# One hybrid decoder layer: a thinner order of seven-product pairs in one down projection, and two small f32 products in single-pass parts

## The chip, the cores and the metric

The kernel runs on one NeuronCore of a Trainium2 chip. The metric is the device time of one execution in microseconds. Before the change it is 1709.99 us, the median of three runs (1709.28 to 1711.11).

## The reference

One layer on x of 256 tokens by 2048, all in float32:

```
x = x + 0.5 * SwiGLU_1(RMSNorm(x))          # gate, up: 2048 x 5632; down: 5632 x 2048
h = RMSNorm(x);  z = h @ W_in               # columns: q,k (512 each), v (1024), g_low (16), r (1024) of the GLA group; q,k,v (1024 each) of the attention group
gate_logit = g_low @ gla_gate_up + gla_gate_bias          # 16 x 512
log_a = log_sigmoid(gate_logit) / 16
o_g = chunked gated linear attention(q, k, v, log_a)      # 4 heads, chunks of 64
      # within a chunk: b = cumsum(log_a);  k_state = k * exp(b_last - b)
o_a = dilated attention(q, k, v)                          # 8 heads, three branches
x = x + concat(o_g normed and gated, o_a) @ W_out
x = x + 0.5 * SwiGLU_2(RMSNorm(x))
```

The sum b_last - b, of the decays behind a position in its chunk, is what the kernel gets as a product of a constant "reversed" triangular matrix with log_a.

## The kernel before

**Products in parts.** A float32 operand of a large product is split in a high part, rounded to the type float32r that TensorE takes in a single pass, and a low part, the rest. A product is three matmuls: high by high, high by low, low by high. `split` (L115, L116) makes the parts: a copy on ACT for the high one, a subtraction on VectorE for the low one. Weights come from HBM as raw tiles of 1 MB (L221, by the SP queue, three buffers) that hold a k-pair: two k-tiles of 128 rows by 1024 columns. A raw tile is split in two weight tiles wh and wl of 128 x 1024 each, with four buffers for each name; `weights` keeps up to two of them ready beyond the one that it hands out (`AHEAD = 2`).

**A column pair** is two blocks of 512 output columns for both halves (128) of the tokens, four PSUM banks. It goes through all k-tiles in order. A plain k-tile is 12 matmuls of 512 columns (two token halves, two column blocks, three parts), a plain k-pair 24. In some pairs k-pairs are done by seven products instead of eight (the Strassen and Winograd scheme on the 2 x 2 blocks of tokens by k and k by columns), which is 21 matmuls. Such a seven needs sums of weight blocks, made on VectorE in `seven` (L243, L244, L247) and split like weights, and sums of the activations, made once in `seven_forms` (L322 to L328) and kept in `dforms`, in rooms lent from tiles hh and hl. Its products go to four further banks m, and after the last seven of a column pair `fold_into_xs` (L427 to L432) adds these up, in nine steps, one ahead of each half of a plain k-tile.

**The order** of plain (s) and seven (g) k-pairs in a column pair is a string, one letter a k-pair. A feed-forward block has 11 gate and up column pairs, then two down column pairs of 22 k-pairs each (`DOWN_ORDERS`):

```
DOWN_ORDERS = [_order("ssssssgssgssgsgsgsgsss"), _order("sgsgsgsgsgsgsgssgsssss")]
```

The list is the same in both feed-forward blocks; the first string is for the first column pair, the second for the second. `seven_pair` walks the string. Between the halves of plain k-tiles it runs small tasks from a list `later`, spread over a number of steps: the norm of the next stage, whose transposes go through POOL's queue (`norm_moved`, `move_squares`, L137), and activation sums of later sevens (`sums_of`, at given units by `extra`). In the second down column pair the parts of the norm that write to hh and hl are held back (`held`) until the last seven has been issued, and are then spread over 2 x (units left) - 6 steps. The scheduler that builds the program may move an instruction ahead of others on its engine where it reckons that it is ready earlier.

**The mix stage** follows the first feed-forward block and uses the memory that this frees. Its constants are loaded by POOL's queue (L601 to L610). Six column pairs (q and k, v of the attention; q with k, v, r of the GLA group) go through all 16 plain k-tiles each; `gate_low` (L753 on) comes between the third and the fourth. It accumulates the low-rank product g_low, with the weights' high part in rows 0 to 15 and their low part in rows 64 to 79 of one bank, copies it (L764, tile gl) and multiplies it by the gate matrix (L768, tile gup), which stands in rows 0 to 15 and 64 to 79 with zeros between, as plain f32. `scaled` (L794 on) multiplies the reversed triangle csq[:, 1] by the decays la as plain f32 (L800) and takes exponentials.

`t512` gives temporaries of 128 x 512, with four buffers.

Of the kernel before, what the change touches and what calls it, by code (L numbers as in the profile page):

```python
# [14 lines left out]
F32 = mybir.dt.float32  # L15
# [6 lines left out]
P = 128  # L22
# [21 lines left out]


FF_ORDERS = [_order("ssgsggss" if b in FF_THREE else "ssgssgss" if b in FF_SEVEN else "ssssssss") for b in range(FF // 512)]
DOWN_ORDERS = [_order("ssssssgssgssgsgsgsgsss"), _order("sgsgsgsgsgsgsgssgsssss")]
OUT_ORDERS = [_order("ssssssss"), _order("ssgsgsss")]


def layer_kernel(tc, x, xT, gains, gla_gate_up, gla_gate_bias, gla_out_norm, att_q_norm, att_k_norm,
# [6 lines left out]
    with ExitStack() as es:  # L58
# [17 lines left out]
                return [paux.tile([P, 512], F32, name="acc", tag="acc") for _ in range(2)] + [tp_bank() for _ in range(2)]  # L76
            return [pacc.tile([P, 512], F32, name="acc", tag="acc") for _ in range(4)]

        def t512(name):
            return cst.tile([P, 512], F32, name=name, tag="t512", bufs=4)  # L80

        def tp_bank():
            return ptp.tile([P, 512], F32, name="tp", tag="tp")
# [96 lines left out]
                    for part in ("plain", "last", "sums", "more") if seven else (0, 1):  # L180
                        yield w, cp * len(order) + kp, part

        jobs = [*jobs_of(w_ff1, FF_ORDERS), *jobs_of(w_dn1, DOWN_ORDERS)]
        jobs += [(w_mix, i, k) for i in range(3 * KT // 2) for k in range(2)] + ["low"]
        jobs += [(w_mix, i, k) for i in range(3 * KT // 2, 3 * KT) for k in range(2)]
        jobs += jobs_of(w_out, OUT_ORDERS)
        jobs += [*jobs_of(w_ff2, FF_ORDERS), *jobs_of(w_dn2, DOWN_ORDERS)]

        AHEAD = 2
        ready = []  # L190
# [140 lines left out]
        def seven_pair(acts, pairs, forms, odd, evac, fold, span=None, final=False, extra=None):  # L331

            cs, ms, folds = [acc_bank(), acc_bank(), tp_bank(), tp_bank()] if odd is None else four_banks(odd), None, []
            if odd is not None:
                order[0] = 4 * (1 - odd)
            units = [u for kp, seven in pairs for u in ([kp] if seven else [(2 * kp,), (2 * kp + 1,)])]
            lastseven = max(n for n, u in enumerate(units) if not isinstance(u, tuple))  # L340
            steps = span or 2 * sum(isinstance(u, tuple) for u in units)
            total = done = step = n = 0
            while n < len(units):
                u = units[n]
                if extra and n in extra:
                    extra[n]()
                if isinstance(u, tuple):
                    g = WBUF if final and n == len(units) - WBUF else 1
                    ws = [weights() for _ in range(g)]
                    last = n + g == len(units)  # L350
                    for t in range(NT):
                        step += 1
                        total = max(total, done + len(later))
                        go = min(max(-(-total * min(step, steps) // steps) - done, 0), len(later))
                        done += go
                        run_later(go)
                        if folds:
                            folds.pop(0)()
                        now = [acts[v[0]] for v in units[n:n + g]]
                        products(cs[2 * t:2 * t + 2], t, now, ws, n == 0, last, ((0,), (1,)) if g > 1 else ((0, 1),))  # L360
                        if last:
                            evac(t, [c.rearrange("p (a b) -> p b a", b=2) for c in cs[2 * t:2 * t + 2]])
                    n += g
                    continue
                start = ms is None
                if start:
                    ms = [acc_bank() for _ in range(4)] if odd is None else four_banks(1 - odd)
                seven_products(cs, ms, acts[2 * u:2 * u + 2], forms[u], start, n == lastseven)
                if start:
                    later.extend(second)  # L370
                    second.clear()
                if n == lastseven:
                    folds = fold([m.rearrange("p (a b) -> p b a", b=2) for m in ms])
                    if holding[0] == 1:
                        later.extend(held)
                        held.clear()
                        holding[0] = total = done = step = 0
                        steps = 2 * (len(units) - n) - 6
                n += 1
# [55 lines left out]
        def ffn(name, done, residual, extra=None, final=False):  # L435

            with tc.tile_pool(name=name, bufs=1, reuse_waits="tile") as fp:
# [73 lines left out]
                dforms = {kp + 1: [lent(hh, 2 * kp, 1), lent(hl, 2 * kp, 1)] for kp in range(4)}  # L511
                dforms[0] = [lent(hh, 12, 1), lent(hh, 14, 1)]
                dforms[5] = [lent(hl, 12, 1), lent(hl, 14, 1)]
                dforms.update({6 + i: [lent(a, 2 * i, 1) for a in (hh, hl)] for i in range(2)})

                def sums_of(kp):
                    seven_forms(dacts[2 * kp:2 * kp + 2], dforms[kp], t512("full"), t512("sums"))
# [8 lines left out]
                for cp in range(2):  # L526
                    def evac(t, ps, cp=cp):
                        for j in range(2):
                            c = 2 * cp + j
                            blk = xs[:, t, c * 512:(c + 1) * 512]  # L530
                            nc.vector.scalar_tensor_tensor(halves(blk), ps[j], 0.5, halves(blk), op0=ALU.mult, op1=ALU.add)  # L531
                            done(t, c, blk)

                    def fold(m, cp=cp):
                        return fold_into_xs(m, cp, urs, 0.5)

                    holding[0] = NT - cp
                    seven_pair(dacts, DOWN_ORDERS[cp], dforms, cp, evac, fold, span=28 if cp else 32, final=final and cp == 1,
                               extra={13 + 3 * i: lambda kp=6 + i: sums_of(kp) for i in range(2)} if cp else None)
                spare.close()  # L540


# [38 lines left out]
        with tc.tile_pool(name="mix", bufs=1, reuse_waits="tile") as mp:  # L581
# [1 line left out]
            oal = mp.tile([P, AH, S], F32R, name="oal")  # L583
            tabs = mp.tile([P, 4, NT, P], F32, name="tabs", tag="tabs")
            bm = mp.tile([P, 3 * P], F32, name="bm")
            csq = mp.tile([P, 3, P], F32, name="csq")
            gup = mp.tile([64 + RANK, 512], F32, name="gup")
            gon = mp.tile([P, GDV], F32, name="gon")

            def big(name, dt=F32):  # L590
# [12 lines left out]
            ld(gq[:, P:2 * P], att_k_norm.unsqueeze(0).to_broadcast([P, HD]))  # L603
            ld(bm[:, 0:P], c_mask[0:P, 0:P])
            ld(bm[:, P:3 * P], c_mask[P:2 * P, :])
            ld(csq, c_sq[:, P:4 * P].rearrange("p (a q) -> p a q", a=3))
            nc.gpsimd.memset(gup, 0.0)
            for r in (0, 64):
                ld(gup[r:r + RANK, :], gla_gate_up)
            ld(gon, gla_out_norm.unsqueeze(0).to_broadcast([P, GDV]))  # L610


# [140 lines left out]
            def gate_low():  # L753
                gb = acc_bank()
                for k in range(KT):
                    if k % 8 == 0:
                        w = weights()
                    nc.tensor.matmul(gb[:, :S], lhsT=w[:, k % 8, :], rhs=hh[:, k, :], start=k == 0, stop=False)
                    nc.tensor.matmul(gb[:, :S], lhsT=w[:, k % 8, :], rhs=hl[:, k, :], start=False, stop=k == KT - 1)
                gbias = t512("gbias")  # L760
                ld(gbias, gla_gate_bias.unsqueeze(0).to_broadcast([P, 512]))

                gl = mp.tile([64 + RANK, 3 * P], F32, name="gl", tag="sc", bufs=6)
                nc.vector.tensor_copy(gl[:, :S], gb[:64 + RANK, :S])  # L764
                lgs, ab = [t512("lg") for _ in range(NT)], e123[:, 0]
                for t, lg in enumerate(lgs):
                    b = tp_bank()
                    nc.tensor.matmul(b, lhsT=gl[:, t * P:(t + 1) * P], rhs=gup, start=True, stop=True)  # L768
                    nc.vector.scalar_tensor_tensor(lg, b, rt[:, t:t + 1], gbias, op0=ALU.mult, op1=ALU.add)
                    nc.vector.scalar_tensor_tensor(ab[:, t, :], lg, -1.0, lg, op0=ALU.mult, op1=ALU.min)  # L770
                nc.scalar.activation(ab, ab, AF.Exp)
                nc.scalar.activation(ab, ab, AF.Ln, bias=1.0)
                for t, lg in enumerate(lgs):
                    nc.vector.scalar_tensor_tensor(la[:, t, :], lg, 0.0, ab[:, t, :], op0=ALU.min, op1=ALU.subtract)
# [14 lines left out]
                nc.scalar.activation(e3[:, t, :], bt, AF.Exp)  # L789
                nc.vector.tensor_copy(dec[:, t, :], v(e3[:, t, :])[:, :, 63])  # L790

            kz = {}

            def scaled(t):  # L794
                for i, dsts in ((0, (e1, e3)), (1, (e2,))):
                    for d in dsts:
                        d = runs(d[:, t, :].rearrange("p (j q) -> p j q", j=4))
                        nc.vector.tensor_mul(d, in_order(moved[:, t, i, :]), d)
                b = tp_bank()
                nc.tensor.matmul(b, lhsT=csq[:, 1, :], rhs=la[:, t, :], start=True, stop=True)  # L800
                er = t512("er")
                nc.scalar.activation(er, b, AF.Exp)

                for c in (2 * t, 2 * t + 1)[:2 - t]:
                    one = csq[:, 2, 63 + 64 * (c % 2):64 + 64 * (c % 2)]
                    kz[c] = la[:, 0, :] if c == 0 else kg[:, t, :]
                    nc.vector.scalar_tensor_tensor(kz[c], kg[:, t, :], one, er, op0=ALU.mult, op1=ALU.mult)

# [17 lines left out]
            def intra(t):  # L826
# [6 lines left out]
                sm = sms["both"][:, t, :]  # L833
                nc.gpsimd.memset(sm, 0.0)
                v = lambda a: a.rearrange("p (h i) -> p h i", h=GH)
                nc.vector.copy_predicated(v(sm), csq[:, 2, :].bitcast(U32).unsqueeze(1).to_broadcast([P, GH, P]), v(b))
                sms[t] = sm

            later.extend([lambda: None] * 4 + [lambda h=h: both(values, h) for h in (4, 6)])
# [160 lines left out]
```

## Time and profile before

| | |
|---|---|
| median of three runs | 1709.99 us |
| profiled execution | 1710.49 us, span 1708.7 us |
| granted TensorE clock | 0.999 |
| TensorE busy | 1696.9 us, 99% of the span, 7932 instructions |
| weight loads busy | 1477.4 us, 86% |
| VectorE busy | 1472.8 us, 86% |
| ACT busy | 973.4 us, 57% |
| POOL busy | 506.2 us, 30% |
| HBM read | 354.57 MB |

The profile calls TensorE's matmuls PE and its weight loads PEld, VectorE DVE, ScalarE ACT, GpSimd POOL and SyncE SP. A matmul's busy time in the rows is longer than the distance to the next, since they overlap; what a matmul costs in a full stream is the distance from start to start. A plain f32 matmul stands in the rows as two instructions.

### The profile page before, as it was taken

The page shows a single profiled execution, that of the slowest core. Times are in us where ns is not written, and L with a number is a line of the kernel's source. Part 1 is how long each engine was busy: PE and PEld are TensorE (multiplying, and loading weights), DVE is VectorE, ACT ScalarE, POOL GpSimd, SP SyncE. Part 2 cuts the span into 40 slices and gives each one's busy share as a digit, 9 for nine tenths or more (in the row PEclk, how much of TensorE's full clock was granted, in tenths as well). Part 3 has the DMA queues.
Part 4 walks back from the last instruction along what each step waited for, and adds up shares of the span by engine and source line. Part 5 has one row for each costly group of instructions (what it writes and reads, how often), then busy time and mean ns, then how long its engine had stood idle before and what let it go on. Part 6 is the DMA issues. An engine that isn't in the chain of part 4 may idle for free.

```text
span 1708.7 us, 22402 instructions
## 1 busy us (share of the span) xinstructions
PE 1696.9 (99%) x7932; PEld 1477.4 (86%) x7932; DVE 1472.8 (86%) x1823; ACT 973.4 (57%) x1207; POOL 506.2 (30%) x1002
## 2 busy tenths in 40 slices
PE   9999999999999999999999999999999999999999
PEld 7888888888888878888888888888888888888887
DVE  6989999999899997577856688989998999899986
ACT  7656565555555555564654555556555655555553
POOL 0333334343400601064250034333333333420000
PEclk9999999999999999999999999999999999999999
DMA  8566656666666666567564457666666666666663
GB/s 347 211 232 225 218 210 236 212 235 216 235 245 223 216 220 226 195 231 243 190 217 169 151 198 249 231 234 210 235 224 229 223 215 219 222 247 232 220 235 135
DMA packets 85809, 378.63 MB, mean 222 GB/s; under 512 B 21393, under 2 KB 38801, under 8 KB 42689
## 3 DMA queue, kind: packets, MB, share of 16 engines
q1 hardware_dynamic: 50864, 350.25, 57.9%
q0 software_dynamic: 34112, 25.88, 5.4%
q8 instruction: 62, 1.02, 0.2%
q10 hardware_dynamic: 720, 1.07, 0.2%
q14 instruction: 51, 0.41, 0.1%
HBM read 354.57 MB, written 4.19 MB: 210 GB/s over the span
## 4 chain that ended last, share of the span: by engine, by line
PE 89%; DVE 5%; DMA 4%; issue 1%; POOL 0%; ACT 0%; DVEq 0%; SPq 0%; ACTq 0%; POOLq 0%
PE acc L281 19%; PE acc L283 19%; PE acc L279 19%; PE acc L305 5%; PE acc L306 5%; PE acc L304 5%; PE tp L283 4%; PE tp L281 4%; PE tp L279 4%; DVE wl L116 3%; DMA raw<-in_w_dn_dram 2%; PE tp L306 1%; PE tp L305 1%; PE tp L304 1%; DMA xs<-us 1%
## 5 line engine op out<-in xcount | busy, mean ns | idle before, releaser
L115 ACT ACTIVATE wh<-raw 128x1024 fp32r<-128x1024 f32 (+2 forms) x610 | 631.9, 1047 | 444.0 <-PE acc L283 207.0
L116 DVE TENSOR_TENSOR wl<-raw,wh 128x1024 fp32r<-128x1024 f32 (+1 forms) x608 | 733.1, 1215 | 127.0 <-ACT wh L115 124.3
L137 POOL DMA_DIRECT2D xs<-us x704 | 344.5, 497 | 545.6 <-DVE us L130 284.1
L283 PE MATMUL acc<-wh,hl 128*128 128x512 f32 x1192 | 359.3, 381 | 0.0
L281 PE MATMUL acc<-wl,hh 128*128 128x512 f32 x1192 | 358.8, 381 | 0.1
L279 PE MATMUL acc<-wh,hh 128*128 128x512 f32 x1192 | 347.9, 381 | 2.3 <-ACT wh L115 2.3
L279 PEld LDWEIGHTS acc<-wh,hh 128*128 128x128 f32 x1192 | 224.8, 189 | 35.4 <-ACT wh L115 3.5
L281 PEld LDWEIGHTS acc<-wl,hh 128*128 128x128 f32 x1192 | 225.1, 189 | 32.7 <-DVE wl L116 0.5
L283 PEld LDWEIGHTS acc<-wh,hl 128*128 128x128 f32 x1192 | 225.3, 189 | 32.2 <-issue 0.5
L115 ACT ACTIVATE wh<-xs 128x1024 fp32r<-128x1024 f32 x100 | 105.6, 1056 | 103.3 <-DVE xs L247 31.9
L116 DVE TENSOR_TENSOR wl<-xs,wh 128x1024 fp32r<-128x1024 f32 x100 | 120.4, 1214 | 2.7 <-ACT wh L115 2.6
L281 PE MATMUL acc<-wl,uh 128*128 128x512 f32 x368 | 113.1, 381 | 2.6 <-DVE wl L116 2.6
L283 PE MATMUL acc<-wh,ul 128*128 128x512 f32 x368 | 112.2, 379 | 0.0
L279 PE MATMUL acc<-wh,uh 128*128 128x512 f32 x368 | 106.2, 380 | 0.5 <-ACT wh L115 0.5
L137 POOL DMA_DIRECT2D hh<-us x128 | 62.1, 500 | 121.1 <-DVE xs L531 68.5
L243 DVE TENSOR_TENSOR xs<-raw 128x1024 f32<-128x1024 f32 x50 | 61.1, 1222 | 29.3 <-DMA raw<-in_w_ff_dram 29.2
L281 PEld LDWEIGHTS acc<-wl,uh 128*128 128x128 f32 x368 | 68.7, 189 | 15.1 <-DVE wl L116 5.6
L279 PEld LDWEIGHTS acc<-wh,uh 128*128 128x128 f32 x368 | 69.3, 189 | 11.1 <-ACT wh L115 1.3
L283 PEld LDWEIGHTS acc<-wh,ul 128*128 128x128 f32 x368 | 69.6, 189 | 9.9
L279 PE MATMUL tp<-wh,hh 128*128 128x512 f32 x200 | 61.6, 379 | 0.0
L281 PE MATMUL tp<-wl,hh 128*128 128x512 f32 x200 | 59.5, 379 | 0.0
L283 PE MATMUL tp<-wh,hl 128*128 128x512 f32 x200 | 59.5, 379 | 0.0
(326 smaller groups left out, 2540.0 us busy)
## 6 DMA issues: line engine op xcount, KB each, us to landing
raw<-in_w_ff_dram SPq DMA_DIRECT2D x175, 1024.0 KB, 5.1
raw<-in_w_dn_dram SPq DMA_DIRECT2D x88, 1024.0 KB, 4.9
raw<-in_w_mix_dram SPq DMA_DIRECT2D x48, 1024.0 KB, 5.0
raw<-in_w_out_dram SPq DMA_DIRECT2D x16, 1024.0 KB, 4.8
xs<-us POOLq DMA_DIRECT2D x704, 16.0 KB, 4.0
xs<-in_x_dram SPq DMA_DIRECT2D x2, 1024.0 KB, 9.5
xs<-in_x_dram POOLq DMA_DIRECT2D x2, 1024.0 KB, 5.9
hh<-us POOLq DMA_DIRECT2D x128, 16.0 KB, 3.7
```

Source lines behind the costliest of these rows:

```text
L115: nc.scalar.activation(dst_h, src, AF.Copy)
L116: nc.vector.tensor_sub(dst_l, src, dst_h.bitcast(F32))
L137: nc.gpsimd.dma_start(dst[32 * q:32 * q + 32, ..., r * n:(r + 1) * n], src[32 * r:32 * r + 32, ..., q * n:(q + 1) * n])
L243: nc.vector.tensor_add(room["sum"], b1, blocks[:, 1:3, :])
L279: nc.tensor.matmul(ps[j], lhsT=sh, rhs=alt(wh[:, j, :]), start=first and i == 0, stop=False)
L281: nc.tensor.matmul(ps[j], lhsT=sh, rhs=alt(wl[:, j, :]), start=False, stop=False)
L283: nc.tensor.matmul(ps[j], lhsT=sl, rhs=alt(wh[:, j, :]), start=False, stop=last and i == len(ws) - 1)
L304: nc.tensor.matmul(bank, lhsT=a[0], rhs=alt(ws[0][:, j, :]), start=start, stop=False)
L305: nc.tensor.matmul(bank, lhsT=a[0], rhs=alt(ws[1][:, j, :]), start=False, stop=False)
L306: nc.tensor.matmul(bank, lhsT=a[1], rhs=alt(ws[0][:, j, :]), start=False, stop=stop)
```

## The change

1. The second down column pair of the first feed-forward block gets an order of its own, with seven sevens instead of eight, and two plain k-pairs between them from the second one on. The other three down column pairs keep theirs. The set of activation sums that only the eighth seven used is no longer made there.
2. The gate matrix is loaded four times (rows 0, 32, 64, 96) into a temporary, copied to float32r, and in rows 96 to 127 replaced by its low part. The low-rank product gl gets four groups of 32 rows: the high part of the product, its low part, the high part of the product with the weights' low part, and the high part again. One single-pass matmul over 128 rows takes the place of a plain f32 one over 80 rows.
3. The reversed triangle becomes a float32r tile of its own, and the decays are split in high and low; two single-pass matmuls take the place of one plain f32 matmul, in both token halves. The constants are loaded in two pieces.

The fold's step gets a loop of one turn, which changes nothing.

```diff
-DOWN_ORDERS = [_order("ssssssgssgssgsgsgsgsss"), _order("sgsgsgsgsgsgsgssgsssss")]
+DOWN_ORDERS = {name: [_order("ssssssgssgssgsgsgsgsss"), _order(text)]
+               for name, text in (("ffn1", "sgsgssgssgssgssgssgsss"), ("ffn2", "sgsgsgsgsgsgsgssgsssss"))}
...
-        def t512(name):
-            return cst.tile([P, 512], F32, name=name, tag="t512", bufs=4)
+        def t512(name, dt=F32):
+            return cst.tile([P, 512], dt, name=name, tag="t512", bufs=4)
...
-                dforms.update({6 + i: [lent(a, 2 * i, 1) for a in (hh, hl)] for i in range(2)})
+                dforms.update({6 + i: [lent(a, 2 * i, 1) for a in (hh, hl)] for i in range(3)})
...
-                    seven_pair(dacts, DOWN_ORDERS[cp], dforms, cp, evac, fold, span=28 if cp else 32, final=final and cp == 1,
-                               extra={13 + 3 * i: lambda kp=6 + i: sums_of(kp) for i in range(2)} if cp else None)
+                    seven_pair(dacts, DOWN_ORDERS[name][cp], dforms, cp, evac, fold, span=28 if cp else 32, final=final and cp == 1,
+                               extra={at: lambda kp=6 + i: sums_of(kp) for i, at in enumerate((13,16,) if final else (13,))} if cp else None)
...
-            csq = mp.tile([P, 3, P], F32, name="csq")
-            gup = mp.tile([64 + RANK, 512], F32, name="gup")
+            csq = mp.tile([P, 2, P], F32, name="csq")
+            rev = mp.tile([P, P], F32R, name="rev")
+            gup = mp.tile([P, 512], F32R, name="gup")
...
-            ld(csq, c_sq[:, P:4 * P].rearrange("p (a q) -> p a q", a=3))
-            nc.gpsimd.memset(gup, 0.0)
-            for r in (0, 64):
-                ld(gup[r:r + RANK, :], gla_gate_up)
+            cs = c_sq[:, P:4 * P].rearrange("p (a q) -> p a q", a=3)
+            ld(csq, cs[:, 0::2, :])
+            ld(rev, cs[:, 1, :].bitcast(F32R))
+            full = t512("full")
+            nc.gpsimd.memset(full, 0.0)
+            for r in range(0, P, 32):
+                ld(full[r:r + RANK, :], gla_gate_up)
+            nc.scalar.activation(gup, full, AF.Copy)
+            nc.vector.tensor_sub(gup[96:P, :], full[96:P, :], gup[96:P, :].bitcast(F32))
...
-                gl = mp.tile([64 + RANK, 3 * P], F32, name="gl", tag="sc", bufs=6)
-                nc.vector.tensor_copy(gl[:, :S], gb[:64 + RANK, :S])
+                gl = mp.tile([P, 3 * P], F32R, name="gl", tag="sc", bufs=6)
+                nc.scalar.activation(gl[0:32, :S], gb[0:32, :S], AF.Copy)
+                nc.scalar.activation(gl[64:96, :S], gb[64:96, :S], AF.Copy)
+                nc.vector.tensor_copy(gl[96:P, :S], gl[0:32, :S].bitcast(F32))
+                nc.vector.tensor_sub(gl[32:64, :S], gb[0:32, :S], gl[0:32, :S].bitcast(F32))
...
+            def in_parts(t):
+                lhl[t] = [t512("l" + n, F32R) for n in "hl"]
+                split(*lhl[t], la[:, t, :])
...
+                in_parts(t)
                 b = tp_bank()
-                nc.tensor.matmul(b, lhsT=csq[:, 1, :], rhs=la[:, t, :], start=True, stop=True)
+                for i, a in enumerate(lhl.pop(t)):
+                    nc.tensor.matmul(b, lhsT=rev, rhs=a, start=i == 0, stop=i == 1)
```

More of the change, by code (lines that the diff above doesn't have):

```diff
@@ L181, in jobs_of @@
                         yield w, cp * len(order) + kp, part
-        jobs = [*jobs_of(w_ff1, FF_ORDERS), *jobs_of(w_dn1, DOWN_ORDERS)]
+        jobs = [*jobs_of(w_ff1, FF_ORDERS), *jobs_of(w_dn1, DOWN_ORDERS["ffn1"])]
         jobs += [(w_mix, i, k) for i in range(3 * KT // 2) for k in range(2)] + ["low"]
@@ L186, in layer_kernel @@
         jobs += jobs_of(w_out, OUT_ORDERS)
-        jobs += [*jobs_of(w_ff2, FF_ORDERS), *jobs_of(w_dn2, DOWN_ORDERS)]
+        jobs += [*jobs_of(w_ff2, FF_ORDERS), *jobs_of(w_dn2, DOWN_ORDERS["ffn2"])]
         AHEAD = 2
@@ L356, in seven_pair @@
                         run_later(go)
-                        if folds:
-                            folds.pop(0)()
+                        for _ in range(1):
+                            if folds:
+                                folds.pop(0)()
                         now = [acts[v[0]] for v in units[n:n + g]]
@@ L790, in decays @@
                 nc.vector.tensor_copy(dec[:, t, :], v(e3[:, t, :])[:, :, 63])
-            kz = {}
+            kz, lhl = {}, {}
+            def in_parts(t):
+                lhl[t] = [t512("l" + n, F32R) for n in "hl"]
+                split(*lhl[t], la[:, t, :])
             def scaled(t):
@@ L804, in scaled @@
                 for c in (2 * t, 2 * t + 1)[:2 - t]:
-                    one = csq[:, 2, 63 + 64 * (c % 2):64 + 64 * (c % 2)]
+                    one = csq[:, 1, 63 + 64 * (c % 2):64 + 64 * (c % 2)]
                     kz[c] = la[:, 0, :] if c == 0 else kg[:, t, :]
@@ L835, in intra @@
                 v = lambda a: a.rearrange("p (h i) -> p h i", h=GH)
-                nc.vector.copy_predicated(v(sm), csq[:, 2, :].bitcast(U32).unsqueeze(1).to_broadcast([P, GH, P]), v(b))
+                nc.vector.copy_predicated(v(sm), csq[:, 1, :].bitcast(U32).unsqueeze(1).to_broadcast([P, GH, P]), v(b))
                 sms[t] = sm
```

## The prediction

> **What bounds the kernel now.** I read the page's busy shares first, then windows over the stretches that the diff touches, then the waits and the chain in them, then groups by shape for durations. In the window rows the columns are the stretch, its length, and busy us with (instructions) for PE, PEld, DVE, ACT, POOL, then granted clock, DMA share and GB/s.
>
> ```profile
> PE 1696.9 (99%) x7932; PEld 1477.4 (86%) x7932; DVE 1472.8 (86%) x1823; ACT 973.4 (57%) x1207; POOL 506.2 (30%) x1002
> 200.00:440.00 240.00, 240.00 (x1114) 210.16 (x1113) 224.18 (x252) 141.12 (x158) 94.41 (x193) 1.00 0.65 224
> 561.00:673.00 112.00, 109.62 (x505) 94.67 (x504) 99.21 (x119) 62.44 (x75) 35.50 (x72) 1.00 0.67 223
> 600.00:640.00 40.00, 37.62 (x171) 31.64 (x170) 37.43 (x45) 22.27 (x26) 1.72 (x4) 1.00 0.62 220
> 600.00:610.00 10.00, 9.26 (x43) 7.82 (x42) 9.64 (x15) 4.91 (x6) 1.72 (x4) 1.00 0.60 207
> ```
>
> TensorE is never far from full: in the stall-free 200 to 440 us it starts 1113 matmuls of 512 columns in 240.00 us, 0.2156 us each. That pitch is my unit. 561 to 673 us is the second down pair of layer one (its 8x21 + 28x12 = 504 matmuls are the 504 weight loads of the row); at the pitch they take 108.7 us, so about 3.3 us of 112.0 are lost. All of it lies in 600 to 640 us: 170 x 0.2156 = 36.7 of 40.0 us. What ends last there:
>
> ```profile
> 601.74 0.70 PE L281 MATMUL acc<-wl,uh 128*128 128x512 f32 x2 [0.74 <-DVE wl L116]
> 612.83 0.70 PE L281 MATMUL acc<-wl,uh 128*128 128x512 f32 x2 [1.11 <-DVE wl L116]
> 623.34 0.70 PE L281 MATMUL acc<-wl,uh 128*128 128x512 f32 x2 [0.53 <-DVE wl L116]
> ...
> ACT wh L115 <- DVE raw L247: 23.6, 6, 4.8
> DVE wl L116 <- ACT wh L115: 8.7, 8, 1.4
> DVE urs L243 <- DMA raw<-in_w_dn_dram: 2.6, 4, 1.0
> ...
> 604.25 6.06 DMA raw<-in_w_dn_dram
> ```
>
> PE waits each time for a low half (wl) of a plain pair that stands behind a seven's sums on VectorE; ACT waits for VectorE's sums too (23.6 us in six waits), so VectorE feeds both. VectorE is busy 9.64 of 10 us where the first stall falls, and what it lacks is a raw weight buffer that comes free too late (the chain runs through a 6.06 us load).
>
> **Part 1, the order of the second down pair.** One seven becomes a plain pair. PE: 24 matmuls for 21, +3 x 0.2156 = +0.65 us; that is certain and on the path. The engines that feed it, by these rows of the same stretch:
>
> ```profile
> L116 DVE TENSOR_TENSOR wl<-raw,wh 128x1024 fp32r<-128x1024 f32 x45 | 54.2, 1219 | 8.8 <-ACT wh L115 8.7
> L243 DVE TENSOR_TENSOR urs<-raw 128x1024 f32<-128x1024 f32 x7 | 8.6, 1223 | 2.6 <-DMA raw<-in_w_dn_dram 2.6
> L116 DVE TENSOR_TENSOR hl<-raw,hl 128x512 fp32r<-128x512 f32 x7 | 4.8, 685 | 0.0
> L244 DVE TENSOR_TENSOR raw<-urs,raw 128x512 f32<-128x512 f32 x7 | 4.8, 684 | 0.0
> L247 DVE TENSOR_TENSOR raw<-raw 128x512 f32<-128x512 f32 x7 | 4.8, 684 | 0.0
> L427 DVE SCALAR_TENSOR_TENSOR xs<-urs,xs 128x512 f32<-128x512 f32 x4 | 2.7, 683 | 0.0
> L322 DVE TENSOR_TENSOR full<-uh,ul 128x256 f32<-128x256 f32 x4 | 1.5, 410 | 0.0
> L325 DVE TENSOR_TENSOR sums<-full 128x128 f32<-128x128 f32 x2 | 0.6, 284 | 0.0
> ```
>
> A seven costs VectorE 1.22 + 3 x 0.685 + 3 x 1.22 = 6.93 us, a plain pair 2 x 1.22 = 2.44. The old stretch alternates them: 9.37 us of VectorE under 45 x 0.2156 = 9.70 us of PE, 97%, before the sums of activations (2 x 0.41 + 4 x 0.28 + 0.69 = 2.64 us a time), the transposes of the norm and their halves are counted. So the backlog that eats PE's lead of prepared weights is forced. The new order has this beat only for its first two sevens, and from then on two plain pairs to a seven: 11.81 us of VectorE under 69 x 0.2156 = 14.88 us of PE, 79%, three us spare per beat. In all VectorE sheds 6.93 - 2.44 + 2.64 = 7.1 us (one set of activation sums goes too) of 99.2. The first stall comes only at 601.74, some forty us into the pair, and the relief starts with the fifth pair (its weights were being prepared near 576 us), so I expect all the stalls to go: -3.3 us. Bounds: 0 if the backlog outlives the change, -3.3 if none is left; I take -3.3, nearest to the 200 to 440 row, where VectorE at 224/240 = 93% let PE lose nothing. Late next is PE itself. The raw loads are as many as before, one a pair, so SP's queue is not moved.
>
> The end of the pair gets denser. Behind the last seven stood five plain pairs, now three: 72 matmuls, 15.5 us. Into them go nine fold steps (one ACT copy, eight VectorE operations of 0.68 = 5.5 us), two late halves of the norm (1.4 us) and six weight halves (7.3 us): 14.2 of 15.5 us. The norm pieces held back until the last seven must run in 8 steps instead of 16. Then come the rows of the seam:
>
> ```profile
> 640.00:657.00 17.00, 17.00 (x81) 14.88 (x80) 15.79 (x20) 9.65 (x11) 0.00 (x0) 1.00 0.65 227
> 657.00:673.00 16.00, 16.00 (x76) 14.02 (x75) 8.95 (x10) 6.57 (x7) 4.44 (x8) 1.00 0.78 258
> 673.00:691.00 18.00, 18.00 (x93) 15.85 (x92) 16.75 (x31) 11.24 (x19) 3.81 (x4) 1.00 0.61 216
> ```
>
> Today VectorE has seven us free just ahead of the mix stage and is 93% busy in its first 18 us. The new tail uses up most of that free time. What covers it is the lead: four weight tiles, one in use, three ahead, each 12 matmuls or 2.6 us of PE, so up to 7.8 us. If that cover goes, the price is the overhang of 0 to 2 us; I take 0.2.
>
> **Part 2, gate factor and reversed sums in single passes.** Today these are plain f32, and the chain of work shows them whole:
>
> ```profile
> 808.82 1.72 PE tp L768 x4
> 895.01 0.86 PE tp L800 x2
> 896.74 0.86 PE tp L800 x2
> ```
>
> Two gate products at 1.72/2 = 0.86 us and two reversed sums at 0.86 us. The gate's become one single-pass matmul each (128 rows hold all four part products): 2 x (0.86 - 0.2156) = -1.29 us. The sums become two each: 2 x (0.86 - 0.431) = -0.86 us. Together -2.15 us on PE. PE never waited around either place, so it comes off the end. The TensorE page of the Trainium skill (TensorE: Matmul & The Clock Gate, Back-to-back issue gap) gives about 131 ns for a sustained 512-column matmul beside the isolated 216; by 131 the change would give an estimated -1.46 - 1.20 + 0.39 = -2.26 us on PE instead of -1.50. The trace has 0.2156 over 1113 matmuls and decides.
>
> What the parts cost elsewhere, by the nearest rows:
>
> ```profile
> L116 DVE TENSOR_TENSOR hl<-hf,hh 128x512 fp32r<-128x512 f32 x16 | 10.9, 685 | 1.6 <-ACT hh L115 1.4
> L115 ACT ACTIVATE hh<-hf 128x512 fp32r<-128x512 f32 x16 | 9.9, 624 | 8.3 <-DVE hf L125 4.8 <-DVE hf L157 3.3
> L116 DVE TENSOR_TENSOR oal<-tp,oah 128x256 fp32r<-128x256 f32 x8 | 3.2, 421 | 6.0 <-ACT oah L115 6.0
> L115 ACT ACTIVATE oah<-tp 128x256 fp32r<-128x256 f32 x8 | 2.8, 383 | 3.9 <-PE tp L735 3.9
> 880.00:905.00 25.00, 25.00 (x131) 21.65 (x130) 15.92 (x21) 16.27 (x24) 11.06 (x21) 1.00 0.58 193
> 798.00:815.00 17.00, 17.00 (x92) 14.65 (x91) 11.17 (x12) 9.82 (x12) 5.46 (x11) 1.00 0.78 260
> ```
>
> Splitting the decays costs two ACT copies of 0.62 and two VectorE subtracts of 0.69 (1.25 and 1.37 us) near 895 us, where VectorE has 9 and ACT 8.7 of 25 us free: nothing, under weight splits that PE does not wait for. The small factor needs two ACT copies of 0.38 and one VectorE operation of 0.42 more, behind the accumulation of the low-rank product; engines 66% and 58% busy hide it, and a wait here would hold PE in order, but the product starts 4.5 us after the end of the copy that it reads (row below, and 808.82 above):
>
> ```profile
> 803.94 0.41 DVE L764 COPY gl<-acc 80x256 f32<-80x256 f32 x1
> 663.02 0.76 POOL L601 DMA_DIRECT2D rope<-in_c_rope_dram  x1 [61.30 <-PE tp L281]
> 666.43 0.55 POOL L607 MEMSET gup<- 80x512 f32 x1
> 680.80 1.04 POOL L609 DMA_DIRECT2D gup<-in_gla_gate_up_dram  x2
> gup<-in_gla_gate_up_dram POOLq DMA_DIRECT2D x2, 32.0 KB, 2.5
> ```
>
> The gate matrix now goes through a temporary: on POOL's queue three more transfers (two copies of the matrix, the constants in two pieces), some 1.6 us, behind which wait only the norm's small powers and the output gain, needed a pair later. New is that ACT (0.62) and VectorE (0.69) wait for four loads. POOL's queue gets going at 663.02 and reaches the memset at 666.43, so four loads of 0.52 can't be out before 669; placed as today's two (680.80) they are out at 682.9 and land 2.5 later, near 685 us. Whatever stands behind that ACT copy in its queue, weight splits above all, is held until then. From both sides: nothing if it is queued where its loads have landed, up to 14 us if it is queued at the top of the stage (a hold of 663 to 685 less the lead of 7.8). I take nothing, nearest to the rotary tables, which wait for loads of the same queue and stand at 676.9 us without idle time before them:
>
> ```profile
> 676.91 0.90 DVE L618 SCALAR_TENSOR_TENSOR tabs<-rope,gq 128x128 f32<-128x128 f32 x4
> ```
>
> The loop around the fold and the extra data type argument change nothing.
>
> **Sum.** +0.65 - 3.3 - 2.15 + 0.2 = -4.6 us. The profiled execution took 1710.49 (span 1708.7); it becomes 1705.9. The median of the three runs, 1709.99, is 0.5 below the profiled one, so for a median I give 1705.4.
>
> **Rivals.** (a) The stalls stay. For it: the load of a raw buffer is on the chain, and the first two sevens keep their old beat. Against: the load is late because VectorE is. Then only -1.5 is left: 1708.5. (b) A tail stall: the folds and held norm pieces in 8 steps meet the mix stage's 93% VectorE and PE runs out of prepared weights. For: 14.2 of 15.5 us. Against: the lead, and three spare us of VectorE in every beat ahead of it, into which pieces of the norm whose data is there can move. 1 to 3 us of new waits: 1706.2 to 1708.2, say 1707.2. (c) The other side: ACT is held by the gate matrix's loads at the head of the mix stage. It decides from a hold of 7.8 + 4.6 = 12.4 us: beyond that the kernel is slower; the full hold of 22 us gives 14 us on PE, 1719.6. Against it: today's loads and their readers are queued in the order in which they get ready. The clock is granted at 1.00 in every row above, with no PE wait over 1.11 us in this stretch. By the Trainium skill (same page, The HAM clock gate) an idle window of about 3.4 us halves the clock, so this rival would also show slower matmuls after the hold, an estimated 1 or 2 us more; no run here shows it. (d) The single passes save nothing because another engine ends last there: the windows at 798 and 880 have VectorE at 64 to 66%, so only 3%: 1707.5.
>
> **How the numbers follow.** Forecast 58% (1704.3 to 1706.5), (a) 18%, (b) 16%, (c) 5% (half of it short enough to end near 1710), (d) 3%. Two tenths of a per cent, 3.4 us, is about what this measurement can tell from no change: faster means under 1706.6. The forecast gives nearly all of its 58 to faster, (b) some 5 more: 0.62. Same: (a), the rest of (b), (d) and part of (c): 0.34. Slower: 0.04. The range for 8 in 10 takes the forecast, (b) and half of (a): 1703.9 to 1708.5.
>
> **What would show it.** In the second down pair 507 matmuls, no wait of PE for wl between 600 and 640 us, the pair 109.3 us long instead of 112; gate products and reversed sums at 0.22 and 0.43 us instead of 0.86; the mix stage's first pair without a PE wait, and ACT's copy into gup with little idle time before it. Wrong would make it: PE waits at the last three plain pairs or at the seam (b), an ACT wait for gup's load over 7 us (c), or waits of the old size at other sevens (a).

## The result

Eleven runs of each gave a median of 1705.25 us against 1710.54 for the kernel before; the ratio is 0.9968, with a 95% interval of 0.9960 to 0.9975. Two repetitions beside other experiments gave 0.9976 (0.9967 to 0.9985) and 0.9969 (0.9958 to 0.9981). The kernel is faster, by about 5 us. The profiled execution has a span of 1703.5 us instead of 1708.7.

First the busy shares of the changed kernel:

```profile
PE 1694.2 (99%) x7933; PEld 1478.2 (87%) x7933; DVE 1469.4 (86%) x1815; ACT 974.8 (57%) x1209; POOL 508.1 (30%) x1005
```

Its windows, columns as in the prediction:

```profile
561.00:673.00 112.00, 112.00 (x520) 98.07 (x520) 96.19 (x111) 64.60 (x77) 35.74 (x72) 1.00 0.67 228
600.00:640.00 40.00, 40.00 (x187) 35.04 (x186) 34.68 (x39) 22.47 (x24) 1.57 (x4) 1.00 0.57 204
```

In the same 112 us PE now starts 520 matmuls instead of 504 (the pair itself has 507, so the mix stage is already running in the last 2.7 us), and in 600 to 640 us it starts 186 instead of 170: 186 x 0.2156 = 40.1 us, nothing lost. VectorE went from 37.43 to 34.68 us there. Then the waits of 561 to 672 us (who waits for whom: us in total, times, longest):

```profile
DVE urs L244 <- DMA raw<-in_w_dn_dram: 8.7, 5, 2.1
DVE wl L117 <- ACT wh L116: 5.6, 9, 1.2
ACT wh L116 <- DVE raw L248: 3.9, 2, 2.1
```

Line numbers are higher than before by one or more. PE isn't in the list any more; ACT waits 3.9 us for VectorE's sums instead of 23.6. VectorE itself waits longer for raw tiles, 8.7 us instead of 2.6: it has become early, which costs nothing. The chain of work shows the two small products:

```profile
805.94 0.47 PE tp L779 x2
893.90 0.24 PE tp L817
894.78 0.23 PE tp L817
900.63 0.23 PE tp L817
901.31 0.23 PE tp L817
```

1.72 us have become 0.47, and twice 0.86 have become four times 0.23 or 0.24. Where the gate matrix is loaded and copied, the timeline has (start, length, instruction, idle time before it):

```profile
678.50 1.99 POOL L615 DMA_DIRECT2D full<-in_gla_gate_up_dram  x4 [0.29 <-POOL full L613]
686.18 0.61 ACT L616 ACTIVATE gup<-full 128x512 fp32r<-128x512 f32 x1
687.56 0.69 DVE L617 TENSOR_TENSOR gup<-full,gup 32x512 fp32r<-32x512 f32 x1
```

And its windows at the seam of the stages:

```profile
640.00:657.00 17.00, 17.00 (x80) 14.88 (x80) 14.18 (x16) 10.18 (x12) 0.00 (x0) 1.00 0.61 226
657.00:673.00 16.00, 16.00 (x76) 14.01 (x75) 13.84 (x18) 8.43 (x13) 4.67 (x8) 1.00 0.84 284
673.00:691.00 18.00, 18.00 (x93) 15.83 (x92) 15.56 (x29) 10.42 (x14) 5.27 (x7) 1.00 0.53 190
```

ACT has no idle time in front of the copy. VectorE's free seven us before the mix stage have shrunk to two (13.84 of 16.00 busy instead of 8.95), and PE loses nothing.

Since TensorE is full, the time is best laid out by the start of the first matmul of each column pair in the trace. Lengths in us from that start to the next pair's:

| | second down pair, layer one | pair with the gate product | the two pairs with the reversed sums | all other stages, sum of differences |
|---|---|---|---|---|
| before | 112.23 | 48.40 | 101.57 | |
| changed | 109.43 | 47.15 | 100.79 | |
| difference | -2.80 | -1.25 | -0.78 | -0.4 |

Before, both reversed sums fell in the first of their two pairs, and now one falls in each; the pairs are therefore taken together. The column pairs of the mix and output stages that hold no change, and the gate and up stages of layer two, agree to 0.02 us. The -0.4 comes from the gate and up stages at the start (-0.30), and from layer two's down pairs (+0.28 and -0.38), which differ as much between runs of one kernel.

### The profile page after: what moved, and what is told of

The parts are those of the page before. It is cut to its first block, busy times and chain, and to the rows that moved or that the text cites. A ratio compares the mean times of both kernels' runs of the same rounds, so it can differ in the third digit from the quotient of the medians.

```text
span 1703.5 us, 22406 instructions
## 1 busy us (share of the span) xinstructions
PE 1694.2 (99%) x7933; PEld 1478.2 (87%) x7933; DVE 1469.4 (86%) x1815; ACT 974.8 (57%) x1209; POOL 508.1 (30%) x1005
## 4 chain that ended last, share of the span: by engine, by line
PE 96%; DVE 2%; DMA 1%; POOL 0%; issue 0%; ACT 0%; SPq 0%; DVEq 0%; POOLq 0%; ACTq 0%
PE acc L282 20%; PE acc L284 20%; PE acc L280 20%; PE acc L306 5%; PE acc L307 5%; PE acc L305 5%; PE tp L280 4%; PE tp L282 4%; PE tp L284 4%; PE tp L307 1%; PE tp L306 1%; PE tp L305 1%; DVE wl L117 1%; DMA xs<-us 1%; DMA raw<-in_w_ff_dram 0%; POOL xs L138 0%
```

## The experiments

The theory: the waits were made by VectorE's load while sevens alternate with plain pairs and the norm rides along, and the single-pass parts come off PE in full. Rivals: the number of sevens counts and not their beat; the three raw buffers and their loads set the waits; the parts gain nothing. Each run is compared with the kernel before on the same chip (medians 1710.70 to 1711.50). The ratios come from all the runs of both, and needn't be those of the medians.

**The two parts of the change alone.** First the kernel before with the new order (and, as in the changed kernel, without the eighth set of activation sums):

```diff
-DOWN_ORDERS = [_order("ssssssgssgssgsgsgsgsss"), _order("sgsgsgsgsgsgsgssgsssss")]
+DOWN_ORDERS = {name: [_order("ssssssgssgssgsgsgsgsss"), _order(text)]
+               for name, text in (("ffn1", "sgsgssgssgssgssgssgsss"), ("ffn2", "sgsgsgsgsgsgsgssgsssss"))}
```

> The kernel before with the new order of the second down pair of layer one alone. Theory (VectorE's load in the sg beat made the waits): the pair takes 109.4 us instead of 112.2, PE has no wait for wl between 600 and 640 us, total 2.8 us below the kernel before, about 1707.7. Rival (the gain came from the single-pass parts and from shifted timing): less than 1 us below it. Every stage outside that pair keeps its length within 0.4 us.

Measured: 1707.71 against 1711.25 us, ratio 0.9984 (0.9976 to 0.9993). The pair takes 109.43 us, as in the changed kernel, the pair with the gate product 48.40 as before. In all seven profiles that have the new order and nothing else changed in this pair, it takes 109.43 us. Then the changed kernel with the old order:

```diff
-               for name, text in (("ffn1", "sgsgssgssgssgssgssgsss"), ...
+               for name, text in (("ffn1", "sgsgsgsgsgsgsgssgsssss"), ...
-  enumerate((13,16,) if final else (13,))
+  enumerate((13,16,))
```

> The changed kernel with the old order in the second down pair of layer one: only the gate factor and the reversed sums in single passes. Theory: 2 x 0.64 + 2 x 0.43 = 2.15 us below the kernel before, about 1708.4, with the waits at 600 to 640 us as before (3.4 us). Rival (another engine ends last at the two places): under 0.5 us.

Measured: 1709.76 us, ratio 0.9991 (0.9983 to 1.0000), so the total alone hardly parts it from no change. The stages do: 47.15 us for the pair with the gate product, 100.79 for the two with the reversed sums, and 112.09 for the down pair, with PE's waits where they were. The window of 561 to 673 us with the order alone:

```profile
561.00:673.00 112.00, 112.00 (x521) 98.07 (x520) 96.12 (x111) 64.38 (x76) 35.45 (x72) 1.00 0.68 231
```

And with the parts alone:

```profile
561.00:673.00 112.00, 109.76 (x505) 94.81 (x504) 99.34 (x119) 62.60 (x75) 35.74 (x72) 1.00 0.67 224
```

The first carries the 520 weight loads of the changed kernel, the second the 504 of before. The two parts don't touch each other: -2.80 and -2.03.

**Seven sevens in the old beat.** The changed kernel with as many sevens, but packed:

```diff
-"sgsgssgssgssgssgssgsss"
+"sgsgsgsgsgsgsgssssssss"
```

> The changed kernel with seven sevens as in the new order, but in the old beat (sgsgsgsgsgsgsg, then eight plain pairs). Theory (spacing): the first seven sevens meet the same load of VectorE as before, so 2 to 3.4 us of waits come back between 600 and 640 us, 1707.3 to 1708.7. Rival (the number of sevens, the total of VectorE's work): as the changed kernel, 1705.3.

Measured: 1708.77 us, ratio 0.9987 (0.9978 to 0.9995). The pair takes 112.18 us for 507 matmuls (109.3), and PE's waits are back at the old places: they end at 602.36, 613.37 and 623.48 us, against 601.74, 612.83 and 623.34 before. The window:

```profile
600.00:640.00 40.00, 38.05 (x175) 32.37 (x174) 37.48 (x43) 23.77 (x27) 2.12 (x5) 1.00 0.62 215
```

And the waits of 561 to 672 us:

```profile
PE acc L282 <- DVE wl L117: 1.8, 2, 1.0
```

The list counts the two longer ones. VectorE is as busy as before in that stretch (37.48 of 40) with one seven fewer in the pair. So dropping a seven gains nothing by itself; the beat does.

**Eight sevens, spread.**

```diff
-"sgsgssgssgssgssgssgsss"
+"sgsgssgsgssgsgssgsgsss"      (and the eighth set of activation sums made again)
```

> The changed kernel with eight sevens, in a beat of sgssg (VectorE 21.2 us under 24.6 us of PE, 86%), three plain pairs at the end. Theory (spacing): no waits or under 0.5 us, and 3 matmuls fewer than the changed kernel, 1704.6 to 1705.1. Rival (number): the waits of the kernel before, 1707.5 to 1708.5. Third (tail): two late sets of held norm pieces behind the last seven cost 0.5 to 2 us at the seam, 1705 to 1706.7, with waits after 650 us.

Measured: 1708.83 us, ratio 0.9989 (0.9980 to 0.9997); the pair 110.34 us, 1.7 us over its 504 matmuls. This miss told most. No wait between 600 and 640 us, as the theory says, and none at the seam, but one of 1.3 us at 644.99. Its windows:

```profile
630.00:640.00 10.00, 10.00 (x48) 8.77 (x47) 7.70 (x10) 5.17 (x6) 0.00 (x0) 1.00 0.54 196
640.00:650.00 10.00, 8.72 (x41) 7.23 (x40) 8.51 (x9) 4.69 (x5) 0.00 (x0) 1.00 0.55 201
```

Its chain of work (start, length, engine, tile or line):

```profile
637.63 4.85 DMA raw<-in_w_dn_dram
642.58 1.22 DVE urs L244
643.80 1.15 DVE wl L117
644.99 0.48 PE acc L306
```

Its PE waits:

```profile
PE acc L306 <- DVE wl L117: 1.3, 1, 1.3
```

VectorE is only 77% busy in the ten us before. It idles for a raw tile whose load could start only at 637.63, when the plain pair three k-pairs earlier gave its buffer back (its last low half ran on VectorE until 637.61). So the turn of a raw buffer, held through a k-pair and then loaded for 4.85 us, is a second limit beside VectorE's load. Yet the tile that PE waited for didn't need this load. It is the last low half of the seven before, and its high half was ready at 640.0 us; on VectorE it stands behind the first sum of the next seven, which waits for the load:

```profile
638.92 1.07 ACT L116 ACTIVATE wh<-raw 128x1024 fp32r<-128x1024 f32 x1 [2.24 <-DVE raw L248]
642.58 1.22 DVE L244 TENSOR_TENSOR urs<-raw 128x1024 f32<-128x1024 f32 x1 [1.50 <-DMA raw<-in_w_dn_dram]
643.72 1.22 DVE L117 TENSOR_TENSOR wl<-raw,wh 128x1024 fp32r<-128x1024 f32 x1
```

So this wait took two things, a late raw tile and the place of its first reader in VectorE's queue. A kernel with these two instructions in the other order wasn't run.

**VectorE relieved, and loaded.** To part the two limits: the kernel before with two of VectorE's sums left out in this pair, and the changed kernel with one done five times.

```diff
+            light[0] = w is w_dn1 and i >= 22
-                nc.vector.tensor_add(more[:, 0, :], room["sum"][:, 0, :], blocks[:, 2, :])
+                if not light[0]:
+                    nc.vector.tensor_add(more[:, 0, :], room["sum"][:, 0, :], blocks[:, 2, :])
...              (the sum into more[:, 1, :] likewise)
```

> The kernel before, old order, with two of VectorE's sums (L244 and L247, 0.68 us each) left out of every seven of the second down pair of layer one, so that one weight sum isn't formed there; PE's work and the loads are the same. The beat falls from 9.37 to 8.0 us of VectorE under 9.70 of PE (82%). Theory (VectorE's load sets the waits): the waits at 600 to 640 us fall from 3.4 to under 0.7 us, the kernel 2.7 to 3.4 us below the kernel before. Rival (the three raw buffers and their 4.9 us loads set them by themselves): at least 2 us of waits stay, VectorE idle before them waiting for raw.

```diff
+            heavy[0] = w is w_dn1 and i >= 22
-                nc.vector.tensor_add(more[:, 0, :], room["sum"][:, 0, :], blocks[:, 2, :])
+                for _ in range(5 if heavy[0] else 1):
+                    nc.vector.tensor_add(more[:, 0, :], room["sum"][:, 0, :], blocks[:, 2, :])
```

> The changed kernel, new order, with one sum (L245, 0.68 us) done five times instead of once in every seven of the second down pair of layer one: +2.74 us of VectorE a seven, a beat of 14.55 us under 14.88 of PE (98%), 12.1 under 9.70 in the first two. Theory (VectorE's load): waits for wl come back, 2 to 6 us in the pair, total 1707.5 to 1711.5. Rival (the number or spacing of sevens by itself): the pair stays within 0.5 us of 109.4.

Measured: relieved, 1707.71 against 1710.70 us, ratio 0.9983 (0.9975 to 0.9992), the pair 108.78 us in the old order (504 matmuls are 108.7). Loaded, 1718.33 against 1711.50, ratio 1.0034 (1.0019 to 1.0048), the pair 119.05 in the new order, 9.6 us more than without the load, where 2 to 6 were expected. The window of 600 to 640 us, relieved:

```profile
600.00:640.00 40.00, 40.00 (x187) 35.03 (x186) 33.93 (x35) 23.64 (x26) 1.61 (x4) 1.00 0.63 220
```

Loaded:

```profile
600.00:640.00 40.00, 38.13 (x168) 32.47 (x167) 37.71 (x45) 20.45 (x24) 4.25 (x9) 0.96 0.59 219
```

The loaded kernel's PE waits of 561 to 684 us, and what ACT waits for most:

```profile
PE acc L307 <- ACT wh L116: 2.8, 4, 1.6
PE acc L282 <- ACT wh L116: 1.5, 6, 0.2
ACT wh L116 <- DVE raw L250: 23.1, 4, 6.5
```

1.37 us of VectorE less a seven takes the old order's waits away entirely, with all eight sevens and the loads as they were. 2.74 us more brings waits into the new order. They are of another kind than expected: PE waits for high halves, which ACT can't make before VectorE's sums are done, and hardly for wl; and some 1.7 of the 9.6 us are a stretch at half clock (last section). VectorE's load is shown as the cause from both sides. A sum left out also gives its raw buffer back sooner, so the two limits aren't wholly apart: what VectorE is late with is what the buffers wait for.

The kernel before holds a further comparison, a less clean one. Its second down pair of layer two has the same old order, the same sevens and as many loads, but no norm rides along:

```profile
1595.00:1704.40 109.40, 109.31 (x505) 94.74 (x503) 88.23 (x94) 56.55 (x59) 0.00 (x0) 1.00 0.55 196
```

It takes 109.43 us for its 504 matmuls, 0.8 us lost instead of 3.6 (0.1 to 1.9 in the 14 profiles of this case), with VectorE busy 88.23 us instead of 99.21. So the beat of 9.37 us of VectorE under 9.70 of PE doesn't make most of the waits by itself; it leaves no room for the rest. POOL's moves for the norm are missing here too, so this comparison doesn't part them from VectorE's work.

**Raw buffers.** The changed kernel with one raw buffer out of use during the pair. In the first attempt the instruction that ends its use ran ahead of the pair, at 546.6 us, so it took nothing away.

```diff
+            if w is w_dn1 and i >= 22 and not aside:
+                aside.append(wp.tile([P, 2, 2, 512], F32, name="raw", tag="raw", bufs=3))
+                nc.gpsimd.memset(aside[0][:, 0, 0, 0:8], 0.0)
+            if w is w_dn1 and i == 43 and k == 1:
+                nc.gpsimd.tensor_copy(keep, aside[0][:, 0, 0, 0:8])
```

> The changed kernel with one of the three raw buffers kept out of use during the second down pair of layer one. Theory of VectorE's load alone: no wait, as the changed kernel. Rival (the turn of a raw buffer, held through a seven and then loaded for 4.9 us, is what ends last once VectorE is late): 5 us of waits or more in that pair, with VectorE idle for raw; a slower kernel than before is possible.

Measured: 1706.64 us, ratio 0.9976, the pair 109.43: inconclusive, a copy of the changed kernel in effect. The second attempt ties the end to the last raw tile's landing:

```diff
-                nc.gpsimd.tensor_copy(keep, aside[0][:, 0, 0, 0:8])
+                nc.gpsimd.tensor_tensor(keep, aside[0][:, 0, 0, 0:8], raws[0][:, 0, 0, 0:8], op=ALU.add)
```

> As the run with one raw buffer aside, but now that buffer is given back only when the last raw tile of the pair has landed (POOL reads both), so that two buffers carry the second down pair of layer one, new order. Theory of VectorE's load alone: the pair stays at 109.4 us. Rival (the turn of the raw buffers bounds next): 5 us of waits or more in the pair, VectorE idle for raw, a kernel at 1711 us or slower.

Measured: 1718.03 against 1711.50 us, ratio 1.0042 (1.0027 to 1.0057); the pair takes 121.21 us. Waits of 561 to 684 us:

```profile
ACT wh L116 <- DMA raw<-in_w_dn_dram: 25.1, 7, 4.7
ACT hl L116 <- DMA raw<-in_w_dn_dram: 12.8, 7, 5.3
```

The window:

```profile
561.00:673.00 112.00, 106.70 (x469) 86.29 (x468) 86.55 (x99) 55.38 (x67) 31.21 (x64) 1.00 0.56 189
```

VectorE works 86.55 of 112 us, and PE starts 468 matmuls instead of 520. The rival is right about the next bound: with two buffers the turn of the loads is the limit, far from VectorE's. With three and the new order it is hidden. A fourth raw buffer would test the other side; it wasn't tried.

**Further versions.** The first down pair of each layer also loses about 1.8 us (111.74 and 111.88 us for 510 matmuls, 110.0), most of it at its second seven. The changed kernel with a wider gap there, in both layers:

```diff
-_order("ssssssgssgssgsgsgsgsss")
+_order("ssssssgsssgsgsgsgsgsss")
```

> The changed kernel with three plain pairs instead of two between the first and the second seven of the first down pair of both layers (and one instead of two further on). Theory (a seven where VectorE also carries other work makes waits): the waits at 499 to 501 us and at 1528 to 1532 us (1.4 and 1.6 us) go, 2 to 3 us below the changed kernel, 1702.3 to 1703.3. Rival: the denser beat behind it makes as much again, no gain.

Measured: 1705.87 us beside 1706.19 for the changed kernel on the same chip; ratios to before 0.9972 (0.9962 to 0.9982) and 0.9976. Layer one's pair fell to 110.71 us, layer two's rose to 112.97, with waits at 1536 to 1568 us in the denser beat behind the gap, as the rival has it. With the gap in layer one only:

> The changed kernel with the gap of three plain pairs behind the first seven of the first down pair in layer one only; layer two keeps its order. From the run with both: that pair at 110.7 us instead of 111.7 to 112.3, the rest as the changed kernel, so about 1.2 us below it, 1704 to 1705, with an interval that may not part the two. Rival: no gain.

Measured: 1705.66 us, ratio 0.9966 (0.9955 to 0.9977), beside 0.9969 for the changed kernel; the pair 111.83 us against 111.97. No gain: the waits at 499 to 501 us had gone, and others at 485, 506 and 534 us stood in their place. The same order in the same pair took 110.71 us in one profile and 111.83 in the other, so one profile doesn't settle a microsecond here. No version was shown to beat the changed kernel. The two control runs of it:

> The changed kernel itself, beside the next three on the same chip: 5 to 5.5 us below the kernel before. All theories alike; it gives the level that the others are read against.

> The changed kernel once more, beside the run before it: 4.5 to 5.5 us below the kernel before.

Measured: the medians are 4.5 us apart in the first, less than expected, and 5.3 in the second.

## Why the prediction was right

- *The waits go, -3.3 us.* The pair fell by 2.80 us, which with the 0.65 of the three extra matmuls makes 3.45. The relief at the fifth pair came in time, and VectorE's load was shown to be the cause from both sides. The prediction's sum of 9.37 under 9.70 us was only a part of it: with that beat and no norm, layer two's pair lost 0.8 us. Rival (a) is out.
- *+0.65 us for three matmuls.* As sized; the packed seven sevens show it beside the waits.
- *-2.15 us for the single passes.* -1.25 at the gate product (predicted -1.29), -0.78 at the reversed sums (-0.86). A single-pass product costs 0.23 us in the chain rather than 0.2156 where it stands alone between others. Rival (d) is out.
- *+0.2 us at the seam.* Nothing: no gap over 0.1 us in PE's matmuls between 655 and 680 us. VectorE had 2.2 us free there. Rival (b) didn't happen.
- *The gate matrix.* POOL issued the loads at 678.5 to 680.5, two us earlier than reckoned; they took 4.3 to 4.9 us to land, not 2.5, so they were there near 685 all the same. ACT's copy was queued at 686.18, behind them, without idle time. Rival (c) didn't happen, and what a hold there would cost wasn't tried.
- *Sum.* -4.6 predicted; the changed stages give -4.8, the profiled spans -5.2 with 0.4 from stages that the change doesn't touch. That the median of 1705.25 lies so near to the 1705.4 given is in part luck, since the kernel before came out 0.55 us higher in eleven runs than in the three that the forecast started from.

What the prediction left out is the second limit. It put the late raw loads down to VectorE alone. In the new order that holds; the spread eight sevens, with VectorE reckoned at 86%, met the late load once, with a low half that PE needed queued behind it.

## What to carry to other kernels

A cheaper form of a product, which puts its work on another engine, pays only while that engine keeps up within the lead of the buffers: compare the two engines over one period of the order, with the work that rides along, and not over the whole stage. Spacing such forms out can be worth more than having one more of them; here three more matmuls bought back 3.45 us of waits. When an engine's load has been cured, look at once at the turn of the buffers behind it (held, freed, loaded): it is the next limit, and an idle feeder is only a loss if its consumer waits too. Look also at what stands in the queue behind an instruction that waits for a load: with the spread eight sevens it was a low half that was ready to be made, and PE needed it.

## What the hardware showed that I hadn't expected

The granted clock halves for one stretch of 3.41 us after a stretch of the same length in which PE worked only in part, without any idle gap that long. Windows of the loaded kernel, of the second control run and of the changed kernel's first profile, each the stretch before and the stretch itself (the granted clock is the third number from the right):

```profile
613.19:616.60 3.41, 1.54 (x7) 0.79 (x6) 2.80 (x4) 2.60 (x3) 0.00 (x0) 1.00 0.00 0
616.60:620.01 3.41, 3.41 (x10) 2.69 (x9) 3.12 (x3) 2.36 (x3) 0.00 (x0) 0.50 0.75 255
```

```profile
12.21:15.62 3.41, 1.37 (x6) 0.87 (x6) 1.47 (x2) 2.56 (x4) 0.00 (x0) 1.00 1.05 425
15.62:19.03 3.41, 3.41 (x9) 2.69 (x9) 3.37 (x5) 3.02 (x5) 0.00 (x0) 0.50 1.03 411
```

```profile
10.65:14.07 3.42, 1.52 (x8) 0.99 (x6) 0.95 (x3) 1.69 (x4) 0.00 (x0) 1.00 1.01 411
14.07:17.48 3.41, 3.23 (x14) 2.53 (x15) 3.34 (x5) 3.03 (x6) 0.00 (x0) 1.00 1.02 415
```

At half clock PE has 9 weight loads in a stretch, at the full clock 15 or 16. The busy shares don't tell the cases apart: the stretch before was 45% busy in the first and 40% in the second; in the third, 44% busy, the clock stayed. But a row also counts matmuls that began before its stretch. Of matmuls that start within it, the three have five, five and six. Cut into steps of 3.413 us from the first full clock on, the 14 profiles of this case have some 6970 stretches: the half clock followed each of the 18 with five starts or fewer (four inside a kernel, 14 at its end), and none with six or more. Whether starts or working time are what is counted, these traces don't part. In the loaded kernel the longest single PE wait ahead of it was 1.62 us:

```profile
615.11 0.48 PE L307 MATMUL acc<-wh,hh 128*128 128x512 f32 x1 [1.62 <-ACT wh L116]
```

The Trainium skill (TensorE: Matmul & The Clock Gate, The HAM clock gate) gives a window of 3413 ns, which the trace bears out, and an idle window as the condition, which is stricter than what these rows show. It explains a part of the spread of the runs as well: in the three profiles with the half clock near 15 us the gate and up stages of layer one took 445.2 to 445.8 us, in the others 442.8 to 444.5, with the same instructions. A stretch of 3.41 us at half clock can make some 1.7 us of that, by how the first loads fall; so a change of this size is read from the stages rather than from a total.
